# Half of the last gate by TensorE inside the attention stage, and five sums of squares in one PSUM tile

## The chip, the cores and the metric

The kernel runs on one core of one Trainium2 chip. The metric is the device time of one execution in microseconds (us); the fewer the better. PE is the engine of matrix products (TensorE; PEld its loads of stationary operands), DVE the vector engine, ACT the scalar engine, POOL the GpSimd engine; SP issues most of the transfers.

## What is computed

One layer of a hybrid diffusion backbone, in float32, on 512 latent tokens and 128 context tokens (640 rows of 1024 features, handled as five tiles of 128 tokens). Each of the two token kinds has a conditioning vector, and six modulation rows come from it:

```python
mod = (silu(cond) @ w_ada + b_ada)            # w_ada: 1024 x 6144
sh1, sc1, g1, sh2, sc2, g2 = split(mod, 6)
h = rms(x, norm_mix) * (1 + sc1) + sh1
q, k, v, gb, gc, u = split(h @ w_in)          # attention, 8 heads of 64; short convolution
attn = softmax(q_r @ k_all.T / 8) @ v_all     # latents read context and latents
y_conv = gb * conv3(gc * u)
x = x + g1 * (concat(rms(attn), rms(y_conv)) @ w_out)
h2 = rms(x, norm_ffn) * (1 + sc2) + sh2
x = x + g2 * ((silu(gate) * up) @ w_down)     # gate, up = split(h2 @ w_gate_up)
```

The edit concerns `g2`, the last of the six pieces ("section 5" of `w_ada`), and the sums of squares inside `rms(y_conv)`.

## The kernel before

Every float32 product is done as three products of rounded halves (`wh`, `wl` are the high and low part of a weight block, `mH`, `mL` of an activation tile, `hH`, `hL` of the normed input), so a "block" of weights is loaded by a transfer, split by one ACT and one DVE operation, and then used by PE.

The stages, in order of time: first norm and the query projection (0 to about 57 us); keys, values and attention (57 to 256); the output projection in two halves of the columns, `j = 0` and `j = 1` (256 to about 325); the feed-forward part in four groups of blocks (to the end). PE's order is written out by hand: the string `SEQ` lists the steps of the attention stage, where `S`, `T`, `O` are scores, transposes and value products of an attention unit, and `F1` takes one step from a list of fillers. The fillers are the matmuls of the gated convolution, twelve blocks (`gc`, `u`, `gb` for each of four tiles `ct` of channels), six steps each, and between them "ada" steps, which work on the pieces of `w_ada` that are due later. The order on the other engines and on SP's queue is set by a scheduler from dependences and priorities (`early(n)` moves an operation forward).

An ada entry is half a section (512 columns). It takes two ada steps: each uses two blocks `aw` of 512 KB (a ring of two buffers), four matmuls of 32 rows by 512 columns, into one PSUM tile. After the second, ACT copies the tile to `rs`; the next step first turns that into what is needed. For section 2 (`g1`) that is a transfer of the bias row into `rs` and two 128x512 products with `selT`; for sections 3 and 4 four narrow products with `sel`. There were six entries, (2,0) to (4,1); the last of them ends in the output projection, where `next(ada_gen)` and `conv_rms()` are called after the 24 matmuls of the first token tile.

Section 5 (`g2`) was done elsewhere. Its first half took four blocks from the ring `wf`, eight times two operations on DVE (`g2_step(0, ...)`, tile `aacc`) beside the first token tiles of `j = 0`, and after the first tile of `j = 1` two products with `ones` and two additions of the broadcast bias `bb` (`g2_out(0)`). Its second half is done in the same manner in the feed-forward part and stays there.

`conv_rms` makes, for each of five token tiles, one product of `ysum` with a column of ones into a PSUM tile of tag `c` (two buffers in that stage), then scale and add on DVE and a power on POOL.

PSUM has eight banks. The attention stage has tags `t` 2, `c` 3, `o` 1 and `s` (two banks) 1; the output projection `t` 2, `c` 2, `s` 2 of two banks each. In `j = 1`, tile by tile: 24 matmuls, then `h2_turn` of the tile before (eight transposes of `x2n`), while ACT, DVE and POOL carry the projected tile through `mix`, `x2`, its sum of squares and `x2n`.

Of the kernel before, what the change touches and what calls it, by code (L numbers as in the profile page):

```python
# [9 lines left out]
F32 = mybir.dt.float32  # L10
# [5 lines left out]
P = 128  # L16
# [3 lines left out]
NT = 5  # L20
# [39 lines left out]
G2P = -300  # L60
CRP = '0e'
# [30 lines left out]
def build(ctx, tc, x_prompt, x_sample, c, cache_k, cache_v, c_ctx, norm_mix, norm_ffn, w_ada, b_ada,  # L92
# [66 lines left out]
    def rstd_of(ss, n, scale, extra=None, tag="rs"):  # L159
        """(ss * scale + eps) ** -0.5 (times extra)"""  # L160
        w = ss.shape[1]
        ms = T("ms", (P, w), F32, 4)
        dve.tensor_scalar(ms, ss, scale, EPS, ALU.mult, ALU.add)
        r = T(tag, (P, w), F32, 6)
        pool.tensor_tensor(r, ms, neghalf[:, :w], ALU.pow)
        if extra is not None:
            dve.tensor_scalar_mul(r, r, extra)
        return r

    open_pool("A", "left", "")  # L170
    open_pool("F", "right", "of y oz ysum m0 g1 rs5 cp")
    open_pool("H", "right", " ".join(f"hH{k} hL{k}" for k in range(KD)))
    open_pool("B1", "left", "t2 tab selT identr ck cv")
# [21 lines left out]
    def op_load(e):  # L195
        """one stationary operand of a gate and up block: a quarter of the block, or a sum of quarters"""
        f, name = e[0][1:]
        g, u = (order[place[x, f]][5] for x in "gu")
        a11, a12, a21, a22 = g[:, 0:4], g[:, 4:8], u[:, 0:4], u[:, 4:8]
        if name[0] == "S":  # L200
            if name == "S1":
                sums[f] = T("sx", (P, 2, 4, P), F32, 2)
            s13, s24 = sums[f][:, 0], sums[f][:, 1]
            src, x, y, op = {"S1": (s13, a21, a22, ALU.add), "S2": (s24, s13, a11, ALU.subtract),
                             "S3": (s13, a11, a21, ALU.subtract), "S4": (s24, a12, s24, ALU.subtract)}[name]
            with early(SOP[f >= NPLAIN]):
                (pool if f < SPO else dve).tensor_tensor(src, x, y, op)
        else:
            src = {"A11": a11, "A12": a12, "A21": a21, "A22": a22}[name]
        w = T(("wh", "wl")[ops[0] % 2], (P, 2, 4, P), F32R, WHB)  # L210
        ops[0] += 1
        with early(SOP[f >= NPLAIN]):
            split(w[:, 0], w[:, 1], src)
        e[5] = w
# [53 lines left out]
    ADA = [(2, 0), (2, 1), (3, 0), (3, 1), (4, 0), (4, 1)]  # L268
# [6 lines left out]
    for n, (off, ct) in enumerate(CONV + [(None, 0)]):  # L275
        if off is not None:
            plan(("conv", off, ct), wi[:, :, off + ct * P:off + (ct + 1) * P])
        for sec, j, h in ada_steps[2 * n:2 * n + 2 if off is not None else None]:
            col = sec * D + j * 512
            plan(("ada", sec, j, h), wa[:, 2 * h:2 * h + 2, col:col + 512], 1, "a")  # L280
    for j in range(2):
        for kp in range(4):
            plan(("o", j, kp), wo[:, 2 * kp:2 * kp + 2, j * 512:(j + 1) * 512], 2 * j, "w", V_AON + 2 * kp)
        for kp in range(0 if j else 4):
            plan(("ada", 5, j, kp), wa[:, 2 * kp:2 * kp + 2, 5 * D + j * 512:5 * D + (j + 1) * 512], 2, "f")
# [32 lines left out]
    def ada1_load(k):  # L318
        """w_ada of feature tile k of the first norm's scale and shift"""
        out = []  # L320
        for h in range(2):
            wf = T("af", (P, 4, 2, P), F32, AFB)
            for i, col in enumerate((D + k * P, k * P)):
                sp.dma_start(wf[:, :, i], wa[:, 4 * h:4 * h + 4, col:col + P])
            out.append(wf)
            yield
        ada1[k] = out
        yield
# [42 lines left out]
    # products with the two conditions: four contraction tiles at a time on the four column groups of the  # L371
    # array, each with its conditions in the first columns; the groups' sums are added by sel afterwards
# [12 lines left out]
    def vec_do():  # L385
        vps = PB((P, 64))
        pe.transpose(vps, rows, ident[:64, :64])
        dve.tensor_copy(vec[:, 0:64], vps)
        # (1 + b_sc) * norm for both norms
        for i, (bo, no) in enumerate(((8, V_MIX), (32, V_FFN))):  # L390
            dve.scalar_tensor_tensor(nb[:, i], vec[:, bo:bo + KD], 1.0, vec[:, no:no + KD], ALU.add, ALU.mult)

# [4 lines left out]
    def mod_evict(i, f0, n, ps_sc, ps_sh):  # L397
        """ps_*: [P, n, 2] sums without bias for features f0..f0+n tiles"""
        no = (V_MIX, V_FFN)[i]
        bo = (0, 24)[i]  # L400
        if ps_sc is not None:
            tmp = T("modt", (P, n, 2), F32, 2)
            dve.tensor_tensor(tmp, ps_sc, vec[:, no + f0:no + f0 + n].unsqueeze(2).to_broadcast([P, n, 2]), ALU.mult)
            dve.tensor_tensor(modA[i][:, f0:f0 + n, :], tmp,
                              nb[:, i, f0:f0 + n].unsqueeze(2).to_broadcast([P, n, 2]), ALU.add)
        if ps_sh is not None:
            dve.tensor_tensor(modB[i][:, f0:f0 + n, :], ps_sh,
                              vec[:, bo + f0:bo + f0 + n].unsqueeze(2).to_broadcast([P, n, 2]), ALU.add)

# [24 lines left out]
    def xT_do(t):  # L434
        """the normed tokens of tile t, feature-major"""
# [144 lines left out]
    def head_norm(ps, nh, t, which):  # L580
        """rms over each head, gain, rotary; ps [P, nh*64] -> SBUF f32 [P, nh, 64]"""
# [86 lines left out]
    # (chunk, columns of the chunk, token columns, columns of the padded row)  # L668
# [17 lines left out]
    def conv_steps(ct):  # L686
# [22 lines left out]
        for i, _ in enumerate(conv_mm(O_GB, ct, bps)):  # L709
            for j, sc, st, sz in PIECES:  # L710
                if i % 3 == 2 and j == i // 3:
                    s1 = slice(sz.start - 1, sz.stop - 1)
                    dve.tensor_tensor(t1[:, s1], bps[j][:, sc], t1[:, s1], ALU.mult)
            yield
        ysq = ysum if ct == 0 else T("c25", (P, PADW), F32, 3)[:, :PADW - 2]
# [6 lines left out]
    def ada_all():  # L722
        for sec, j in ADA:
# [10 lines left out]
            if sec == 2:  # L734
                sp.dma_start(res[2:3], b_ada[0:1, sec * D + j * 512:sec * D + (j + 1) * 512])
            yield
            if sec == 2:
                for cc in range(2):
                    ps = PB(tag="c")
                    pe.matmul(ps, selT[:, cc], res, start=True, stop=True)  # L740
                    act.activation(g1[cc][:, j * 512:(j + 1) * 512], ps, AF.Copy)
# [18 lines left out]
    def conv_rms():  # L760
        for t in range(NT):
            sps = PB((P, 1), tag="c")
            c0 = t * P + (2 if t == CTX else 0)
            pe.matmul(sps, ysum[:, c0:c0 + P], ones[:, 0:1], start=True, stop=True)
            rB[t] = rstd_of(sps, 1, 1.0 / 512, tag="rB")

    filler = itertools.chain(*(conv_steps(ct) for ct in range(4)), ada_some(12))
    NFILL = 12 * 6 + 12
# [76 lines left out]
    def att_add(t, v, e):  # L845
        # the rows of the v lo products go to the other half of the partitions
# [13 lines left out]
    # the context tokens' queries: four heads at a time  # L860
# [82 lines left out]
    open_pool("D", "right", "mix mH mL aacc bb")  # L943
    phase[0] = 2

# [34 lines left out]
    def g2_step(j, kp):  # L980
        """a quarter of g2's columns: sums over the contraction on the vector engine, then over partitions"""
        w = W(("ada", 5, j, kp))
        for i in range(2):
            k = 2 * kp + i
            for cc in range(2):
              with early(G2P) if G2P and j == 0 else ExitStack():
                if k == 0:
                    g2acc[cc] = T("cg", (P, TOK), F32, 2)[:, :512] if j else T("aacc", (P, 512), F32, 2)
# [4 lines left out]
    def g2_out(j):  # L993
        cols = slice(j * 512, (j + 1) * 512)
        bb = T("cu", (P, TOK), F32, 2)[:, :512] if j else T("bb", (P, 512))
# [6 lines left out]
    # second operands of the gate and up products: quarters of h2 (contraction half, token half) and their sums  # L1002
# [34 lines left out]
    for j in range(2):  # L1037
        cols = slice(j * 512, (j + 1) * 512)
        for n, t in enumerate(TORD[j]):
# [22 lines left out]
            if j == 0 and G2N <= n < 4 + G2N:  # L1062
                g2_step(0, n - G2N)
            if j == 1 and n == 0:
                g2_out(0)
# [18 lines left out]
    # ---- SwiGLU: a gate block and its up block by half the contraction against half the tokens, seven products  # L1084
    # for the eight (Winograd's form) ----
# [16 lines left out]
    def plain(f, bs, toks):  # L1102
        """gate and up blocks of one half of the tokens by plain products"""
# [173 lines left out]
def _rope_constants():  # L1277
    """cos and signed sin of the axial angles, [512 tokens, 64]: they depend on the shapes alone"""
# [37 lines left out]
```

## Time and profile before

| | us |
|---|---|
| median of 3 runs (lowest, highest) | 772.96 (770.6, 773.28) |
| span of the profiled execution, first to last instruction | 771.6 |
| PE busy | 744.2 (96%) |
| DVE busy | 563.1 (73%) |
| ACT busy | 376.8 (49%) |
| POOL busy | 70.8 (9%) |

The profile is of one execution. Its span is 771.6 us; no time of its own beside that is recorded, so what lies around the span is known only as the 1.4 us between it and the median of the runs. The views read here are the shares of the engines, the table by stretches of time (busy time of each engine, granted clock of PE, share and rate of the transfers), the timeline, the chain that ended last, and the answers by tile. In a row of the timeline stand start, duration, engine, line, operation, output and inputs, size and count, and in brackets how long the engine had been idle before it and who ended that.

### The profile page before, as it was taken

To read this page: it belongs to the slowest core of one execution; us is meant where nothing else is said; L and a number is where in the kernel's file an instruction comes from. 1 tells how busy PE (TensorE), PEld (TensorE's weight loads), DVE (VectorE), ACT (ScalarE), POOL (GpSimd) and SP (SyncE) were. 2 spreads that over 40 slices of the span, in tenths; PEclk is the share of its full clock that TensorE was granted. 3 is DMA by queue.
4 is the path that set the end of the run, shared out by engine and by line. 5 is a ranking of instruction groups with operands and counts; after the bars stand their busy time and mean duration, and the time that the engine had idled before them with its cause. 6 is when DMAs were issued, how large, how long until landed. Compare 5 with 4: busy or idle time off the path is not lost.

```text
span 771.6 us, 11961 instructions
## 1 busy us (share of the span) xinstructions
PE 744.2 (96%) x4580; PEld 669.2 (87%) x4580; DVE 563.1 (73%) x1033; ACT 376.8 (49%) x732; POOL 70.8 (9%) x97
## 2 busy tenths in 40 slices
PE   4999999999999999996999999999999999999997
PEld 3778988989999787886998789999889998899986
DVE  5566887675666799789778777984677866788653
ACT  5446676666665346875452125554125542255510
POOL 3105101011010330044100000000000000000000
PEclk9999999999999999999899999999999999999999
DMA  9984134424325433111134412233112231222312
GB/s 290 308 236 128 42 109 140 121 90 140 120 89 171 161 133 110 56 55 55 56 110 153 134 55 83 83 109 110 54 56 82 83 109 56 80 84 84 110 55 82
DMA packets 102350, 84.53 MB, mean 110 GB/s; under 512 B 4526, under 2 KB 82674, under 8 KB 102292
## 3 DMA queue, kind: packets, MB, share of 16 engines
q1 hardware_dynamic: 100980, 83.39, 35.0%
q8 instruction: 36, 0.59, 0.3%
q10 hardware_dynamic: 1056, 0.26, 0.2%
q0 software_dynamic: 256, 0.11, 0.1%
q14 instruction: 22, 0.18, 0.1%
HBM read 79.68 MB, written 2.75 MB: 107 GB/s over the span
## 4 chain that ended last, share of the span: by engine, by line
PE 83%; DVE 8%; ACT 3%; DMA 2%; issue 2%; SPq 2%; POOL 1%; ACTq 0%; POOLq 0%
PE pf L155 17%; PE pf L157 17%; PE pf L156 17%; PE pc L678 3%; PE pc L679 3%; PE pc L680 3%; PE ps L155 3%; PE ps L156 3%; PE ps L157 3%; PE po L833 2%; PE ps L790 2%; PE pt L816 2%; PE pc L380 2%; DMA af<-in_w_ada_dram 2%; DVE wl L152 1%
## 5 line engine op out<-in xcount | busy, mean ns | idle before, releaser
L151 ACT ACTIVATE wh<-wf 128x1024 fp32r<-128x1024 f32 (+1 forms) x76 | 64.1, 843 | 93.1 <-PE pf L157 63.2
L155 PE MATMUL pf<-wh,gH 128*128 128x512 f32 (+1 forms) x225 | 88.2, 392 | 0.0
L157 PE MATMUL pf<-wh,gL 128*128 128x512 f32 (+1 forms) x225 | 87.7, 390 | 0.0
L156 PE MATMUL pf<-wl,gH 128*128 128x512 f32 (+1 forms) x225 | 87.7, 390 | 0.0
L152 DVE TENSOR_TENSOR wl<-wf,wh 128x1024 fp32r<-128x1024 f32 (+1 forms) x42 | 49.4, 1176 | 27.8 <-ACT wh L151 24.9
L678 PE MATMUL pc<-hH,wh 128*128 128x320 f32 x192 | 61.7, 321 | 0.0
L679 PE MATMUL pc<-hL,wh 128*128 128x320 f32 x192 | 60.0, 312 | 0.0
L680 PE MATMUL pc<-hH,wl 128*128 128x320 f32 x192 | 59.9, 312 | 0.0
L155 PE MATMUL pf<-T,wh 128*128 128x320 f32 x160 | 50.1, 313 | 6.2 <-ACT p L1125 6.2
L155 PEld LDWEIGHTS pf<-wh,gH 128*128 128x128 f32 x225 | 42.3, 188 | 9.8 <-ACT wh L151 0.2
L157 PEld LDWEIGHTS pf<-wh,gL 128*128 128x128 f32 x225 | 42.3, 188 | 9.8
L156 PEld LDWEIGHTS pf<-wl,gH 128*128 128x128 f32 x225 | 42.3, 188 | 9.8 <-issue 0.2
L156 PE MATMUL pf<-T,wh 128*128 128x320 f32 x160 | 49.9, 312 | 0.0
L157 PE MATMUL pf<-T,wh 128*128 128x320 f32 x160 | 49.9, 312 | 0.0
L155 PE MATMUL pf<-T,wl 128*128 128x320 f32 x160 | 49.3, 308 | 0.0
L156 PE MATMUL pf<-T,wl 128*128 128x320 f32 x160 | 49.3, 308 | 0.0
L157 PE MATMUL pf<-T,wl 128*128 128x320 f32 x160 | 49.3, 308 | 0.0
L156 PE MATMUL pf<-B,wl 128*128 128x320 f32 x152 | 47.5, 313 | 0.3 <-DVE B L1020 0.3
L155 PE MATMUL pf<-B,wl 128*128 128x320 f32 x152 | 47.4, 312 | 0.0
L157 PE MATMUL pf<-B,wl 128*128 128x320 f32 x152 | 47.2, 310 | 0.0
L1230 DVE TENSOR_TENSOR dm<-pf,g 128x512 f32<-128x512 f32 (+1 forms) x41 | 27.7, 676 | 22.9 <-PE pf L157 22.9
L151 ACT ACTIVATE wl<-wf 128x512 fp32r<-128x512 f32 x34 | 21.4, 630 | 43.5 <-PE pf L156 36.8
(308 smaller groups left out, 2097.5 us busy)
## 6 DMA issues: line engine op xcount, KB each, us to landing
wf<-in_w_gate_up_dram SPq DMA_DIRECT2D x44, 512.0 KB, 3.8
aw<-in_w_ada_dram SPq DMA_DIRECT2D x24, 512.0 KB, 4.7
wf<-in_w_down_dram SPq DMA_DIRECT2D x20, 512.0 KB, 3.2
wf<-in_w_in_dram SPq DMA_DIRECT2D x18, 512.0 KB, 5.9
af<-in_w_ada_dram SPq DMA_DIRECT2D x32, 256.0 KB, 6.1
x<-in_x_sample_dram SPq DMA_DIRECT2D x8, 512.0 KB, 5.3
wf<-in_w_out_dram SPq DMA_DIRECT2D x8, 512.0 KB, 4.5
wf<-in_w_ada_dram SPq DMA_DIRECT2D x8, 512.0 KB, 3.8
```

The costliest lines, as they stand in the source:

```text
L151: act.activation(hi, src, AF.Copy)
L152: dve.tensor_tensor(lo, src, f32(hi), ALU.subtract)
L155: pe.matmul(out, lh, rh, start=start, stop=False, skip_group_check=more)
L156: pe.matmul(out, lh, rl, start=False, stop=False, skip_group_check=more)
L157: pe.matmul(out, ll, rh, start=False, stop=stop, skip_group_check=more)
L380: pe.matmul(out[CG * g:CG * (g + 1)], cp[:, k], w, start=(k < 4), stop=(k >= KD - 4), skip_group_check=True)
L678: pe.matmul(acc, wh[:, k], hH[k][:, c0:c0 + n], start=(k == 0), stop=False)
L679: pe.matmul(acc, wh[:, k], hL[k][:, c0:c0 + n], start=False, stop=False)
L680: pe.matmul(acc, wl[:, k], hH[k][:, c0:c0 + n], start=False, stop=(k == KD - 1))
L790: pe.matmul(s2[:, g, :320], q, kk[:, v, P + g * 320:P + (g + 1) * 320], start=(i == 0), stop=(i == 1))
L816: pe.transpose(tp[:, i, h], u[3][h][:, kt * P:(kt + 1) * P], ident)
L1230: dve.tensor_tensor(dm, ps[:, :n], g2[cc][:, oc], ALU.mult)
```

## The change

The first half of section 5 becomes a seventh ada entry, `(5, 0)`, done on PE like section 2: its bias row goes into `rs`, and two `selT` products give the first halves of the two `g2` tiles, copied by ACT. To have room for it, two ada steps are added: in the `gb` blocks of the channel tiles in `AMID`, 0 and 1, after the first half of the block, with two more `aw` blocks planned there. So every entry comes earlier, the last ada step now stands just ahead of the output projection, and what follows the first token tile there is the end of entry (5,0) in place of (4,1). The DVE path for that half, its `aacc` and `bb` tiles, its four `wf` loads and its two products with `ones` go. `conv_rms` puts its five sums into one PSUM tile of tag `t` and makes one DVE and one POOL operation of them. `selT` moves to a pool that lives longer.

```diff
+AMID = (0, 1)
-    ADA = [(2, 0), (2, 1), (3, 0), (3, 1), (4, 0), (4, 1)]
+    ADA = [(2, 0), (2, 1), (3, 0), (3, 1), (4, 0), (4, 1), (5, 0)]
...
+    for off, ct in CONV:
+        plan(("conv", off, ct), wi[:, :, off + ct * P:off + (ct + 1) * P])
+        n = 4 if off == O_GB and ct in AMID else 2
+        at += n
+        for sec, j, h in ada_steps[at - n:at]:
             col = sec * D + j * 512
             plan(("ada", sec, j, h), wa[:, 2 * h:2 * h + 2, col:col + 512], 1, "a")
...
-        for kp in range(0 if j else 4):
-            plan(("ada", 5, j, kp), wa[:, 2 * kp:2 * kp + 2, 5 * D + j * 512:5 * D + (j + 1) * 512], 2, "f")
...
                     dve.tensor_tensor(t1[:, s1], bps[j][:, sc], t1[:, s1], ALU.mult)
             yield
+            if i == 2 and ct in AMID:
+                yield from ada_some(1)
...
-            if sec == 2:
+            if sec in (2, 5):
                 sp.dma_start(res[2:3], b_ada[0:1, sec * D + j * 512:sec * D + (j + 1) * 512])
             yield
-            if sec == 2:
+            if sec in (2, 5):
                 for cc in range(2):
                     ps = PB(tag="c")
                     pe.matmul(ps, selT[:, cc], res, start=True, stop=True)
-                    act.activation(g1[cc][:, j * 512:(j + 1) * 512], ps, AF.Copy)
+                    act.activation((g1 if sec == 2 else g2)[cc][:, j * 512:(j + 1) * 512], ps, AF.Copy)
...
     def conv_rms():
+        sps = PB((P, NT))
         for t in range(NT):
-            sps = PB((P, 1), tag="c")
             c0 = t * P + (2 if t == CTX else 0)
-            pe.matmul(sps, ysum[:, c0:c0 + P], ones[:, 0:1], start=True, stop=True)
-            rB[t] = rstd_of(sps, 1, 1.0 / 512, tag="rB")
+            pe.matmul(sps[:, t:t + 1], ysum[:, c0:c0 + P], ones[:, 0:1], start=True, stop=True)
+        r = rstd_of(sps, NT, 1.0 / 512, tag="rB")
+        for t in range(NT):
+            rB[t] = r[:, t:t + 1]
...
-            if j == 0 and G2N <= n < 4 + G2N:
-                g2_step(0, n - G2N)
-            if j == 1 and n == 0:
-                g2_out(0)
```

Three places show how the built orders differ; the names are tiles with their running numbers, a bracket names whose semaphore an instruction waits for.

On PE, the end of the attention stage before: value products `po`, the last ada step (`aw` with `cp`), the last two value products, then the output projection (`ps`, with the context tile `m`).

```order
L833 MATMUL po_3235<-pl_3208,VS_696 128x256
L380 MATMUL pc_3096<-aw_3097,cp_84 32x512 [waits DMAHW6_49]
L380 MATMUL pc_3096<-aw_3097,cp_84 32x512
L380 MATMUL pc_3096<-aw_3101,cp_84 32x512 [waits DMAHW7_49]
L380 MATMUL pc_3096<-aw_3101,cp_84 32x512
L833 MATMUL po_3235<-ph_3214,VS_696 128x256 [waits Activation_49]
L833 MATMUL po_3235<-pl_3215,VS_696 128x256 [waits DVE_49]
L155 MATMUL ps_3297<-wh_3105,m_170_701 128x512 [waits PE_49]
```

The same place on PE now:

```order
L838 MATMUL po_3245<-pl_3225,VS_696 128x256 [waits DVE_49]
L679 MATMUL pc_3235<-hH_40_155,wh_3013 128x320
L680 MATMUL pc_3235<-hL_48_163,wh_3013 128x320
L681 MATMUL pc_3235<-hH_40_155,wl_3014 128x320
L679 MATMUL pc_3235<-hH_41_156,wh_3013 128x320
L680 MATMUL pc_3235<-hL_49_164,wh_3013 128x320
L681 MATMUL pc_3235<-hH_41_156,wl_3014 128x320
L381 MATMUL pc_3130<-aw_3131,cp_84 32x512 [waits DMAHW2_49]
L381 MATMUL pc_3130<-aw_3135,cp_84 32x512 [waits DMAHW3_49]
L156 MATMUL ps_3325<-wh_3139,m_170_701 128x512 [waits DVE_49,Activation_49]
```

And on ACT, the rows from the copy of the last value products (`t`) on:

```order
L845 ACTIVATE t_772_3201<-po_3245 128x256 [waits PE_49]
L249 ACTIVATE wh_3183<-wf_3181,vec_143 128x512 [waits DMAHW4_49,PE_49]
L720 ACTIVATE c_782_3280<-y_699 128x512 [waits DVE_49]
L720 ACTIVATE c_782_3280<-y_699 128x128 [waits DVE_49]
L736 ACTIVATE rs_783_3289<-pc_3130 128x512 [waits PE_49]
L152 ACTIVATE mH_3321<-y_699 128x512
```

The last six convolution matmuls have moved behind the last value products, the ada step stands directly ahead of the output projection, and the first `ps` matmul waits for ACT: its tile takes PSUM banks 0 and 1, and bank 0 holds `pc_3130`, the ada step's sum, until the `rs` copy has read it (before, the sum stood in bank 2).

On PE after the first 24 matmuls of the output projection, before:

```order
L157 MATMUL ps_3297<-wh_3138,mL_3294 128x512
L745 MATMUL pc_3328<-sel_140,rs_774_3253 128x2 x4
L764 MATMUL pc_3336<-ones_130,ysum_700 128x1 [waits Pool_49]
L764 MATMUL pc_3342<-ones_130,ysum_700 128x1 [waits DVE_49]
L764 MATMUL pc_3348<-ones_130,ysum_700 128x1 [waits DVE_49]
L764 MATMUL pc_3354<-ones_130,ysum_700 128x1 [waits DVE_49]
L764 MATMUL pc_3360<-ones_130,ysum_700 128x1 [waits DVE_49,Pool_49]
```

and now:

```order
L158 MATMUL ps_3325<-wh_3183,mL_3322 128x512
L743 MATMUL pc_3395<-rs_783_3289,selT_142 128x512 [waits DMAHW0_49]
L743 MATMUL pc_3398<-rs_783_3289,selT_142 128x512
L767 MATMUL pt_3401<-ones_130,ysum_700 128x1 [waits Pool_49]
L767 MATMUL pt_3401<-ones_130,ysum_700 128x1 x3
L767 MATMUL pt_3401<-ones_130,ysum_700 128x1 [waits Pool_49]
L156 MATMUL ps_3426<-wh_3139,mH_3418 128x512 [waits Activation_49]
```

The four narrow `sel` products are replaced by two full `selT` products, and the sums no longer wait for DVE one by one.

On DVE, the first token tile of `j = 1` on its way to `x2n`, before (`mix` scaled, gated, added to `x`; `g` the two bias additions of `g2_out(0)`):

```order
L1072 SCALAR_TENSOR_TENSOR mix_3658<-ps_3615,rA_2009,mix_3658 128x512 [waits Activation_49]
L1000 TENSOR_TENSOR g_784_3291<-pt_3652,bb_3650 128x512 [waits PE_49]
L1074 TENSOR_TENSOR mix_3658<-mix_3658,g_166_697 128x512 [waits DVE_49]
L1000 TENSOR_TENSOR g_785_3292<-pt_3655,bb_3650 128x512 [waits PE_49]
L1075 TENSOR_TENSOR x_837_3466<-mix_3658,x_837_3466 128x512 [waits DMAHW7_49,DVE_49]
L152 TENSOR_TENSOR mL_3740<-y_699,mH_3739 128x512
L152 TENSOR_TENSOR mL_3818<-of_3032,mH_3817 128x512 [waits PE_49,Activation_49]
L163 TENSOR_SCALAR ms_3666<-ss_3664 128x1 [waits Activation_49]
```

and now:

```order
L1072 SCALAR_TENSOR_TENSOR mix_3630<-ps_3595,rA_2015,mix_3630 128x512 [waits Activation_49]
L153 TENSOR_TENSOR mL_3712<-y_699,mH_3711 128x512 [waits PE_49]
L1074 TENSOR_TENSOR mix_3630<-mix_3630,g_166_697 128x512 [waits DVE_49]
L153 TENSOR_TENSOR mL_3790<-of_3042,mH_3789 128x512 [waits PE_49,Activation_49]
L1075 TENSOR_TENSOR x_829_3460<-mix_3630,x_829_3460 128x512 [waits DMAHW2_49,DVE_49]
L164 TENSOR_SCALAR ms_3638<-ss_3636 128x1 [waits Activation_49]
```

The two additions are gone, and the low half `mL` of a later token tile, which waits for ACT's `mH` of it, now stands ahead of the addition to `x`.

More of the change, by code (lines that the diff above doesn't have):

```diff
@@ L170, in build @@
     open_pool("A", "left", "")
-    open_pool("F", "right", "of y oz ysum m0 g1 rs5 cp")
+    open_pool("F", "right", "of y oz ysum m0 g1 rs5 cp selT")
     open_pool("H", "right", " ".join(f"hH{k} hL{k}" for k in range(KD)))
-    open_pool("B1", "left", "t2 tab selT identr ck cv")
+    open_pool("B1", "left", "t2 tab identr ck cv")
     open_pool("B0", "left", "crow rows rows2 res x xT hF af")
@@ L274, in build @@
     ada_steps = [(sec, j, h) for sec, j in ADA for h in range(4)]
[L275 to L278, printed above, removed]
+    at = 0
+    for off, ct in CONV:
[3 more added lines that the diff above has]
+        for sec, j, h in ada_steps[at - n:at]:
             col = sec * D + j * 512
@@ L760, in conv_rms @@
     def conv_rms():
+        sps = PB((P, NT))
         for t in range(NT):
-            sps = PB((P, 1), tag="c")
             c0 = t * P + (2 if t == CTX else 0)
-            pe.matmul(sps, ysum[:, c0:c0 + P], ones[:, 0:1], start=True, stop=True)
-            rB[t] = rstd_of(sps, 1, 1.0 / 512, tag="rB")
-    filler = itertools.chain(*(conv_steps(ct) for ct in range(4)), ada_some(12))
-    NFILL = 12 * 6 + 12
+            pe.matmul(sps[:, t:t + 1], ysum[:, c0:c0 + P], ones[:, 0:1], start=True, stop=True)
+        r = rstd_of(sps, NT, 1.0 / 512, tag="rB")
+        for t in range(NT):
+            rB[t] = r[:, t:t + 1]
+    filler = itertools.chain(*(conv_steps(ct) for ct in range(4)), ada_some(2 * len(ADA)))
+    NFILL = 12 * 6 + 2 * len(ADA)
     used = [0]
@@ L942, in build @@
     open_pool("Y1", "left", "B11 B21")
-    open_pool("D", "right", "mix mH mL aacc bb")
+    open_pool("D", "right", "mix mH mL")
     phase[0] = 2
@@ L985, in g2_step @@
             for cc in range(2):
-              with early(G2P) if G2P and j == 0 else ExitStack():
                 if k == 0:
-                    g2acc[cc] = T("cg", (P, TOK), F32, 2)[:, :512] if j else T("aacc", (P, 512), F32, 2)
+                    g2acc[cc] = T("cg", (P, TOK), F32, 2)[:, :512]
                     dve.tensor_scalar_mul(g2acc[cc], w[:, i], cs[:, k, cc:cc + 1])
@@ L994, in g2_out @@
         cols = slice(j * 512, (j + 1) * 512)
-        bb = T("cu", (P, TOK), F32, 2)[:, :512] if j else T("bb", (P, 512))
+        bb = T("cu", (P, TOK), F32, 2)[:, :512]
         sp.dma_start(bb, b_ada[0, 5 * D + j * 512:5 * D + (j + 1) * 512].partition_broadcast(P))
```

## The prediction

> **What bounds the kernel now.** I read the page first: the shares of the engines and of the chain that ended last.
>
> ```profile
> span 771.6 us, 11961 instructions
> PE 744.2 (96%) x4580; PEld 669.2 (87%) x4580; DVE 563.1 (73%) x1033; ACT 376.8 (49%) x732; POOL 70.8 (9%) x97
> PE 83%; DVE 8%; ACT 3%; DMA 2%; issue 2%; SPq 2%; POOL 1%; ACTq 0%; POOLq 0%
> ```
>
> PE is the bound: 27 us of the span are without it, and its share of the chain is ten times any other's. So work taken from DVE counts only where PE waits for DVE, and work given to PE counts in full unless PE was idle there. The table by stretches (columns: stretch, length, then busy time and instructions of PE, PEld, DVE, ACT, POOL, granted clock, transfer share, GB/s) says where that is:
>
> ```profile
> 98.00:150.00 52.00, 51.88 (x373) 46.34 (x366) 39.88 (x78) 36.41 (x72) 3.79 (x6) 1.00 0.41 129
> 150.00:200.00 50.00, 49.96 (x367) 45.76 (x366) 31.96 (x66) 30.59 (x62) 5.48 (x9) 1.00 0.32 102
> 200.00:256.00 56.00, 56.00 (x415) 51.20 (x414) 37.42 (x76) 33.45 (x68) 2.41 (x7) 1.00 0.38 124
> 262.00:266.00 4.00, 2.63 (x21) 2.43 (x20) 3.94 (x13) 0.94 (x2) 1.42 (x2) 0.98 0.65 212
> 266.00:270.00 4.00, 4.00 (x12) 3.13 (x12) 2.32 (x6) 0.69 (x1) 2.42 (x4) 0.59 0.87 324
> ```
>
> From 98 to 256, where all ada steps stand, PE idles 0.16 us of 158. Right behind the output projection's first tile it idles 1.37 of 4, and in the next 4 us its clock is 0.59. After 325 nothing changes; that part only shifts.
>
> **A. Two more ada steps, four more narrow products ahead of the projection.** Prices from the chain (start, duration, what):
>
> ```profile
> 158.94 1.72 PE pc L740 x4
> 186.20 0.15 PE pc L680
> 186.35 0.79 PE pc L745 x8
> 187.13 0.99 PE pc L380 x8
> 188.71 0.24 PE po L833 x2
> 273.17 0.79 PE pt L902 x8
> ```
>
> One full ada step (two blocks, eight passes) takes 0.99, two 1.98. The `sel` products of entry (4,1), 0.79, move from behind the projection's first tile into this stretch. PE is full there, so both count whole: **+2.77**.
>
> **A'. New waits in that stretch.** The `aw` ring has two buffers, so a step's loads start only when the step before it has been read. Before, their closest spacing was 12.5 us (rows of SP's queue); by the order now, steps 3 to 4, 6 to 7 and 7 to 8 are some 7.2, 7.5 and 6.3 us apart (24 convolution passes at 0.15, eight to ten `po` passes at 0.12, a step's own 0.99, a few scores and transposes).
>
> ```profile
> 231.77 0.89 SPq L225 DMA_DIRECT2D aw<-in_w_ada_dram  x2
> 244.26 0.89 SPq L225 DMA_DIRECT2D aw<-in_w_ada_dram  x2
> DMA to landing us min/median/max: 3.7/4.7/6.4
> PE ps L790 <- ACT pr L798: 0.6, 1, 0.6
> ```
>
> The second block lands about 0.1 + 0.45 + 4.7 = 5.25 us after the release (half of 0.89 until it is issued; the median landing), 6.95 at the longest landing. It is needed in the middle of the next step, so available are 6.7, 7.0 and 5.8 (the spacings less half of 0.99). So normally no wait; with the longest landing 1.15 and 0.25, together 1.4. Since scores and transposes also shift against each other, three unit waits of the size of the last row (1.8) may come on top: bounds 0 and 3.2 (nothing below 0, since that stretch has only 0.16 us of idle to give back). I take **+0.5**, near the low end, because the median landing leaves no wait.
>
> **B. The first projection matmul waits for ACT.** Its two-bank tile now covers the bank that holds the last ada sum, and is written only when ACT has copied that to `rs`. Before, in the timeline:
>
> ```profile
> 253.64 0.31 PE L680 MATMUL pc<-hH,wl 128*128 128x320 f32 x1
> 253.84 0.72 ACT L248 ACTIVATE wh<-wf,vec 128x512 fp32r<-128x512 f32 x1 [1.68 <-PE pc L679]
> 254.74 0.71 ACT L248 ACTIVATE wh<-wf,vec 128x512 fp32r<-128x512 f32 x1
> 255.35 0.82 ACT L717 ACTIVATE c<-y 128x512 f32<-128x512 f32 x2
> 256.07 0.58 ACT L733 ACTIVATE rs<-pc 128x512 f32<-128x512 f32 x1
> ```
>
> Counted from the last convolution pass (253.64): ACT has the `wh` split from +0.20, the second `wh` from +0.83 (0.63 per split, back to back), the two `c` squares from +1.44 (0.61 later, as 254.74 to 255.35), `rs` from +2.16 (0.72 later, as 255.35 to 256.07), done at +2.74. PE is done with that pass and the ada step at about +1.2 (0.15 and 0.99). So it waits about 1.5 to 1.6: **+1.6**; bounds 0 (`rs` goes ahead of the squares and splits) and 2.0 (one more `wh` row, 0.7, less what overlaps).
>
> **C, D, E. The block of sums behind the projection's first tile.**
>
> ```profile
> 259.20 0.40 PE L156 MATMUL ps<-wl,mH 128*128 128x512 f32 x1
> 259.71 0.50 PE L157 MATMUL ps<-wh,mL 128*128 128x512 f32 x1
> 260.05 0.40 PE L155 MATMUL ps<-wh,mH 128*128 128x512 f32 x1
> 262.15 0.95 PE L745 MATMUL pc<-sel,rs 128*128 128x2 f32 x8
> 264.49 0.60 PE L764 MATMUL pc<-ones,ysum 128*128 128x1 f32 x4 [1.16 <-DVE modt L403]
> 265.30 0.61 PE L764 MATMUL pc<-ones,ysum 128*128 128x1 f32 x4 [0.20 <-DVE ms L163]
> 265.76 0.72 PE L155 MATMUL ps<-wh,mH 128*128 128x512 f32 x1
> 269.26 0.39 PE L157 MATMUL ps<-wh,mL 128*128 128x512 f32 x1
> ```
>
> A `ps` pass at full clock takes 0.233 (nine from 260.05 to 262.15). C: a wait for the first `mL` (259.20 to 259.71, 0.28 more than a pass) ends, since DVE gets it during B: **-0.28**. D: from 262.15 to 265.76 are 3.61 us. Now stand there two `selT` products, 1.72, and ten ones-passes at 0.79/8 = 0.099, 0.99, which share one PSUM tile and wait for no DVE: 2.71, so **-0.90** (bounds -0.9 and, if the first `selT` product waits for the bias row's transfer, up to 0). E: from 265.76 to 269.26 eight passes take 3.50 instead of 8 x 0.233 = 1.87, the low clock after the narrow block. With PE denser there: **-1.63** (bounds -1.63 and 0).
>
> **F. First tile of `j = 1`.**
>
> ```profile
> 296.39 1.88 PE L999 MATMUL pt<-aacc,ones 128*128 128x512 f32 x4
> 300.92 0.63 ACT L151 ACTIVATE mH<-of 128x512 fp32r<-128x512 f32 x1 [3.36 <-issue]
> 301.46 1.04 ACT L1080 ACTIVATE x2n<-x 128x1024 f32<-128x1024 f32 x1
> 301.59 0.69 DVE L152 TENSOR_TENSOR mL<-of,mH 128x512 fp32r<-128x512 f32 x1 [0.24 <-ACT mH L151]
> 304.25 1.09 PE L961 MATMUL pt<-ident,x2n 128*128 128x128 f32 x8 [0.37 <-DVE x2n L1082]
> 305.10 0.48 PE L155 MATMUL ps<-wh,mH 128*128 128x512 f32 x1
> ```
>
> Let T be the end of tile 0's matmuls (296.39). Before, the matmuls of tile 2 begin at T+8.71. The products with `ones` are gone (1.72 by the `selT` row), so PE has tile 1 done at T+5.6 (24 x 0.233). But the chain to `x2n` isn't shorter by that: DVE now has `mL` of a later tile ahead of the addition to `x`; it waits for ACT's `mH`, which comes after the 11th matmul of tile 1, at T+2.8 (before, 300.92 = T+4.53, the same 1.72 later). So `mL` from T+3.5, the addition from about T+4.1, ACT's square from T+4.84, the transposes 2.79 later (301.46 to 304.25) at T+7.63, the next matmuls 0.85 after that (304.25 to 305.10), T+8.48: **-0.23**, with a new wait of PE of about 2.0 in place of 1.72 of work and 0.37 of wait. Without `mL` in front it would be about T+6.5; bounds -2.1 (work and wait both gone) and 0.
>
> **G. Off the path, 0:** the 16 DVE products into `aacc` and two bias additions, four short powers on POOL, four `wf` transfers that become four `aw` transfers of the same size on the same queue, the broadcast bias that becomes one row.
>
> ```profile
> L991 DVE SCALAR_TENSOR_TENSOR aacc<-wf,cs,aacc x14: 735/742/1772, 258.3 to 280.6; 128x512 f32<-128x512 f32 x14
> ```
>
> Twelve us of DVE, but from 258 to 281 PE waited for DVE only in the places above; PE's own work covers it, and were it not covered, it would cost nothing to be without it.
>
> **Sum:** 2.77 + 0.5 + 1.6 - 0.28 - 0.90 - 1.63 - 0.23 = +1.83. The profiled span 771.6 becomes 773.4; the median, 1.4 above that span, becomes 772.96 + 1.83 = **774.8**. It is a small sum of larger terms: what is won in the transition is paid in the attention stretch and in two new waits. Half a per cent, 3.9 us, is about what a measurement of this kernel can tell from no change.
>
> **A rule against the rows: the clock.** The rows of E show a drop after 1.36 us of waits within 3.6 us of narrow products. One more place shows it:
>
> ```profile
> 72.00:74.00 2.00, 1.15 (x9) 0.87 (x9) 2.00 (x11) 1.74 (x5) 0.70 (x1) 1.00 0.24 70
> 74.00:76.00 2.00, 2.00 (x13) 2.00 (x14) 1.65 (x5) 1.83 (x5) 0.80 (x1) 0.67 0.00 0
> ```
>
> PE was idle 0.85 of 2 us here, and the clock fell to 0.67. So a drop can follow B (1.6 idle) or F (2.0 idle and eight transposes). The Trainium skill, "TensorE: Matmul & The Clock Gate", section "HAM oscillation — how this bites in real kernels", has as its rule that the array must have no idle gap above some 3.4 us; by that rule neither B nor F lowers the clock and the sum stays at +1.83. Both rows above disagree with it as it stands, since these gaps were shorter; by them the sum could be +3.46.
>
> **Rivals.**
> R1, the low clock comes back at one of the new waits: E's 1.63 is not won (or is paid again), 774.8 + 1.63 = 776.4. For it: the rows at 72 and 266. Against: full matmuls stand on both sides of B and F. Chance 0.22.
> R2, the ada steps arrive late, the other side: the short spacing makes them wait for loads (1.4) and three units slip (1.8), 2.7 above the 0.5 taken: 777.5, slower. It decides from 2.0 above my sum, where 776.8 is passed. For it: spacing down from 12.5 to 6.3 with no third buffer. Against: the median landing. Chance 0.13.
> R3, the waits of B and F don't appear, since ACT gets to `rs` sooner and `x2n` is done as early as PE is free: -1.6 and, to T+6.5 for the transposes' end, some -1.1: 772.1. For it: neither wait is seen in this trace, and both rest on an order of queues. Against: that order is fixed, and the durations are measured. Chance 0.18.
> R1 with R2: 779.1, chance 0.05.
> My forecast, 774.8: 0.42.
>
> **Numbers.** Forecast and R3 and most of R1 lie within 3.9 us: same 0.74. Slower, R2, R1 with R2 and the upper part of R1: 0.23. Faster needs 769.1, below R3; it takes R3 with F's lower bound: 0.03. Range 771.8 (just below R3) to 778.2 (above R2); beyond it are R1 with R2 and an R3 at its bounds, the forecast with another sign of A', under 0.2 in all.
>
> **What would show it.** The stretch up to the projection longer by about 2.8 us with PE still full and waits of ada steps for `aw` under 1.4 in all (A, A'). A wait of about 1.6 before the first `ps` pass, ended by ACT's `rs` copy (B). No waits between the ones-passes, clock 1.0 behind them (D, E). A wait of about 2 us before tile 0's `x2n` transposes, with DVE's `mL` ahead of the addition (F). Wrong I'd be by a clock below 0.9 behind B or F, or by a sum of `aw` waits above 2.

## The result, and the profile after

| | before | after |
|---|---|---|
| median, us (lowest to highest) | 772.61 (770.6 to 773.28) | 779.32 (778.89 to 780.97) |
| span of the profiled execution, us | 771.6 | 778.0 |

The ratio of the times is 1.0085, with a 95% interval of 1.0063 to 1.0107: the kernel became 6.7 us slower, 0.85%. The forecast was 774.8 with a range to 778.2, so the time lies above it.

The page of after, the three lines that answer to those shown of before:

```profile
span 778.0 us, 11967 instructions
PE 747.3 (96%) x4596; PEld 668.5 (86%) x4596; DVE 551.5 (71%) x1011; ACT 378.9 (49%) x735; POOL 66.5 (9%) x93
PE 79%; DVE 9%; ACT 4%; DMA 3%; POOL 2%; issue 2%; SPq 1%; ACTq 0%; DVEq 0%; POOLq 0%
```

DVE has lost 11.6 us of work, as the edit says. PE is busy 3.1 us longer and idle 3.3 us longer, and the chain shows it: four points have gone from PE to DVE, ACT, DMA and POOL. Where is read from the table by stretches. I cut it at the same instructions in both kernels, the first `aw` step and the first `ps` pass of the output projection (first row before, the others after; columns as in the prediction):

```profile
97.79:256.18 158.39, 158.22 (x1154) 143.64 (x1153) 109.66 (x218) 100.85 (x204) 11.75 (x23) 1.00 0.37 119
```

```profile
96.40:264.48 168.08, 163.84 (x1177) 145.40 (x1177) 111.39 (x221) 102.41 (x207) 11.39 (x23) 1.00 0.39 124
72.00:76.00 4.00, 3.02 (x24) 2.74 (x25) 4.00 (x16) 3.56 (x10) 1.37 (x2) 1.00 0.12 35
306.00:310.00 4.00, 2.06 (x11) 1.42 (x10) 2.12 (x5) 2.24 (x4) 0.55 (x1) 1.00 0.00 0
310.00:314.00 4.00, 4.00 (x16) 3.43 (x15) 3.67 (x13) 3.39 (x9) 0.00 (x0) 0.57 0.00 0
```

The stretch grew by 9.69 us, where the prediction had 4.87 (A, A' and B). PE's idle in it went from 0.17 to 4.24. The waits of PE in after, from 96 us to the end of the projection (who waited, for whom; total, times, longest):

```profile
PE pt L966 <- DVE x2n L1082: 1.9, 1, 1.9
PE ps L156 <- ACT rs L736: 1.5, 1, 1.5
PE ps L795 <- ACT pr L803: 1.2, 3, 0.6
PE pc L381 <- ACT c L693: 0.7, 1, 0.7
PE pt L821 <- DVE pl L153: 0.6, 1, 0.6
```

The first two are F and B of the prediction. The other three belong to the attention stage, and none of them is for a transfer: `pr` and `pl` belong to the units, and the ada step that waits for `c` waits for a PSUM buffer that ACT has still to read. Of the 1.2 us for `pr`, one wait of 0.59 ends at 95.6 us, ahead of the stretch; before had the same one there (0.56).

How a unit came to wait is seen at one place. Before, timeline, PE, from the first eight transposes of a unit to its last two:

```profile
157.91 1.04 PE L816 MATMUL pt<-ident,pr 128*128 128x128 f32 x8
158.78 1.88 PE L740 MATMUL pc<-rs,selT 128*128 128x512 f32 x4
160.59 1.06 PE L380 MATMUL pc<-aw,cp 128*32 128x512 f32 x8
161.59 0.44 PE L816 MATMUL pt<-ident,pr 128*128 128x128 f32 x2
```

The same unit after, with DVE:

```profile
160.68 1.03 PE L821 MATMUL pt<-ident,pr 128*128 128x128 f32 x8
161.47 0.39 PE L679 MATMUL pc<-hH,wh 128*128 128x320 f32 x1
162.49 1.28 DVE L153 TENSOR_TENSOR pl<-pt,ph 128x512 fp32r<-128x512 f32 x2
163.23 0.44 PE L821 MATMUL pt<-ident,pr 128*128 128x128 f32 x2 [0.64 <-DVE pl L153]
```

Before, 2.8 us of filler (two `selT` products and an ada step) stood between the two groups of transposes, and DVE's `pl` had emptied the PSUM buffer in time. After, the filler that falls here is six convolution passes, 0.9 us; DVE has emptied it only at about 163.2, and PE waits 0.64. The long filler has moved to another unit, which had shown no wait without it.

The start of the output projection (B), the block of sums (C to E) and the first tile of `j = 1` (F), timeline of after:

```profile
261.94 1.06 PE L381 MATMUL pc<-aw,cp 128*32 128x512 f32 x8
263.85 0.57 ACT L736 ACTIVATE rs<-pc 128x512 f32<-128x512 f32 x1
264.48 0.50 PE L156 MATMUL ps<-wh,m 128*128 128x512 f32 x1 [1.48 <-ACT rs L736]
```

```profile
270.19 1.88 PE L743 MATMUL pc<-rs,selT 128*128 128x512 f32 x4
271.90 1.17 PE L767 MATMUL pt<-ones,ysum 128*128 128x1 f32 x10
272.93 0.48 PE L156 MATMUL ps<-wh,mH 128*128 128x512 f32 x1
274.89 0.40 PE L158 MATMUL ps<-wh,mL 128*128 128x512 f32 x1
```

```profile
305.51 0.69 DVE L153 TENSOR_TENSOR mL<-of,mH 128x512 fp32r<-128x512 f32 x1 [0.34 <-ACT mH L152]
306.12 0.68 DVE L1075 TENSOR_TENSOR x<-mix,x 128x512 f32<-128x512 f32 x1
309.74 1.69 PE L966 MATMUL pt<-ident,x2n 128*128 128x128 f32 x8 [1.94 <-DVE x2n L1082]
311.08 0.78 PE L156 MATMUL ps<-wh,mH 128*128 128x512 f32 x1
```

The wait for the copy to `rs` is 1.48, the block takes 2.74 (270.19 to 272.93), eight passes behind it take 1.96 in place of 3.50, and PE waits 1.94 for `x2n`, with `mL` ahead of the addition to `x`. Behind that last wait the granted clock fell to 0.57 (310 to 314), and the transposes and the passes after them took some 1.6 us longer. Against this, the low clock that before had from 74 us on is missing (72 to 76 at 1.00), though PE's instructions there are the same.

### The profile page after: what moved, and what is told of

The parts are those of the page before. It is cut to its first block, busy times and chain, and to the rows that moved or that the text cites. A ratio compares the mean times of both kernels' runs of the same rounds, so it can differ in the third digit from the quotient of the medians.

```text
span 778.0 us, 11967 instructions
## 1 busy us (share of the span) xinstructions
PE 747.3 (96%) x4596; PEld 668.5 (86%) x4596; DVE 551.5 (71%) x1011; ACT 378.9 (49%) x735; POOL 66.5 (9%) x93
## 4 chain that ended last, share of the span: by engine, by line
PE 79%; DVE 9%; ACT 4%; DMA 3%; POOL 2%; issue 2%; SPq 1%; ACTq 0%; DVEq 0%; POOLq 0%
PE pf L156 17%; PE pf L158 17%; PE pf L157 17%; PE pc L679 3%; PE ps L156 3%; PE pc L680 3%; PE pc L681 3%; PE ps L157 3%; PE ps L158 3%; PE po L838 2%; PE ps L795 2%; PE pc L381 2%; DMA af<-in_w_ada_dram 2%; PE pt L821 2%; POOL rs L166 1%
```

## The experiments

Each was timed in five rounds beside the kernel before; the ratio is to that kernel, with its 95% interval. After itself has 1.0085 [1.0063, 1.0107].

**The shift alone.** The kernel before, with two empty steps:

```diff
+            if i == 2 and ct in (0, 1):
+                yield
...
-    NFILL = 12 * 6 + 12
+    NFILL = 12 * 6 + 14
```

> The kernel before, with all its work, but with two empty filler steps (nothing is done in them) where the change puts its two added ada steps. So every later convolution and ada step stands one or two places later against the attention units, as in the change, and the last six convolution passes and the last ada step stand behind the last value products. Theory 1 (the loss is the displacement: PE's fillers no longer cover the softmax of the units they were placed for): the attention stretch gets some 4 to 5 us longer by waits of single units, and the wait for the copy to rs of 1.5 us appears; 772.6 + 5.5 = about 778. Rival (the loss is the added work, its loads, and its waits for PSUM): only the 1.5 us in front of the output projection appear, about 774.

Measured: 779.29 us, ratio 1.0075 [1.0054, 1.0096]. Its stretch from the first `aw` step to the projection, and PE's waits in it:

```profile
98.87:264.45 165.58, 161.41 (x1154) 144.23 (x1153) 111.39 (x219) 101.81 (x206) 11.38 (x23) 1.00 0.35 114
```

```profile
PE ps L155 <- ACT rs L735: 1.5, 1, 1.5
PE pt L818 <- DVE pl L152: 0.7, 1, 0.7
PE po L835 <- DVE pl L152: 0.6, 2, 0.3
```

The same 1154 passes as before take 165.58 in place of 158.39: 7.2 us longer with nothing added, and 1.48 of that is B. Of the rest, 5.7, some 2.5 is idle that before didn't have (2.7 in place of 0.17); the other 3.2 is longer busy time of the same passes. Most of it stands at the recorded waits themselves, for a wait costs more than its idle: in after the last of the six convolution passes starts at 162.29 and the transposes behind it at 163.23, 0.94 where such a pass takes 0.15, with 0.64 recorded as idle. Counted so, from start to start, the ten unit waits of this run that before didn't have come to some 4.8 of the 5.7 (an estimate from its timeline).

Two kinds of wait have to be told apart. Seven of the ten stand where they stand in after too, most with nearly the same size, as the first row here (0.67; in after 0.64). The other two rows stand where the second empty step is; there after has `sel` products and an ada step, and no wait:

```profile
162.37 0.44 PE L818 MATMUL pt<-ident,pr 128*128 128x128 f32 x2 [0.67 <-DVE pl L152]
172.71 0.39 PE L835 MATMUL po<-ph,VS 128*128 128x256 f32 x1 [0.25 <-ACT ph L151]
173.44 0.38 PE L835 MATMUL po<-pl,VS 128*128 128x256 f32 x1 [0.34 <-DVE pl L152]
```

So about 1 us of this run's loss comes from the step being empty, which the change doesn't have, and the wait of 0.7 us for `c` in after isn't in this run. With that said, the shift is enough to make most of the loss, and it costs more than the added work.

**The added steps without a place of their own.**

```diff
-            yield
-            if i == 2 and ct in AMID:
-                yield from ada_some(1)
+            if i == 2 and ct in AMID:
+                list(ada_some(1))
+            yield
...
-    NFILL = 12 * 6 + 2 * len(ADA)
+    NFILL = 12 * 6 + 2 * len(ADA) - len(AMID)
```

> The change, but each of the two added ada steps is done within the filler step ahead of it and takes no place of its own, so every convolution pass stands against the attention units where it did before. All the work is the same. Theory 1 (displacement): waits in the attention stretch fall from about 5 us to about 1, and the wait ahead of the output projection becomes 0 to 0.8; 779.3 - 4 - 1 = about 774. Rival (added work and loads cost by themselves): 777.5 to 779.

Measured: 777.9 us, ratio 1.0069 [1.0044, 1.0094]: my theory missed by 4 us, and the time is that of the rival. The stretch, a part of it, and its waits:

```profile
96.42:264.73 168.31, 164.19 (x1178) 146.79 (x1177) 110.20 (x220) 101.21 (x206) 12.28 (x23) 0.99 0.39 123
228.00:232.00 4.00, 2.79 (x22) 2.71 (x20) 2.07 (x5) 1.29 (x4) 0.00 (x0) 1.00 0.08 25
232.00:236.00 4.00, 4.00 (x20) 3.96 (x21) 1.41 (x3) 2.42 (x5) 0.70 (x5) 0.58 0.00 0
```

```profile
PE pt L907 <- ACT osq L861: 1.2, 1, 1.2
PE pt L821 <- DVE pl L153: 1.1, 1, 1.1
PE ps L795 <- ACT pr L803: 0.8, 1, 0.8
```

The convolution passes stand where they stood, B is down to 0.4, and still units wait, 3.5 us in all with a wait of 0.4 that the list leaves out, and a low clock follows one of the waits. So the place of the convolution passes isn't all that the loss hangs on. The two steps with an added ada step are longer by it, and what this edit doesn't put back is the ada entries: with two more steps ahead of them, every entry after the first comes a step or two earlier, and with it the long fillers (`selT` 1.7, `sel` 0.8). "Displacement" would have to be taken wider than I had put it: any filler of another length at a unit's gap. That the entries are what is left was not tried by itself. By this run alone the rival, that the added work costs by itself, would stand; what speaks against it is e1, which loses without added work, and e5 below, which has all of it and loses little.

**The sums alone,** on the kernel before: only the new `conv_rms`.

```diff
+        sps = PB((P, NT))
         for t in range(NT):
-            sps = PB((P, 1), tag="c")
...
+        r = rstd_of(sps, NT, 1.0 / 512, tag="rB")
```

> The kernel before with only the other part of the change, the five sums of squares in one PSUM tile. The two waits of PE for DVE (1.36 us) and, if they cause it, the low clock behind them (1.63 us) go: 772.6 - 2.8 = about 769.8. Rival (the drop of the clock comes from the narrow products and not from the waits): 771.3.

Measured: 769.47 us, ratio 0.9955 [0.9939, 0.997]. In before, the longer of PE's two waits in this block (1.16 us) was for `modt`, which on DVE stood behind two products into `aacc`:

```profile
262.94 1.42 DVE L991 SCALAR_TENSOR_TENSOR aacc<-wf,cs,aacc 128x512 f32<-128x512 f32 x2
264.27 0.16 DVE L403 TENSOR_TENSOR modt<-pc,vec 128x8 f32<-128x8 f32 x1
```

The two stretches in which before had 1.37 us of idle and a clock of 0.59, now:

```profile
262.00:266.00 4.00, 4.00 (x28) 3.64 (x27) 3.93 (x10) 0.94 (x2) 0.88 (x1) 1.00 0.51 153
266.00:270.00 4.00, 4.00 (x19) 3.21 (x18) 2.87 (x4) 1.31 (x2) 2.35 (x2) 1.00 0.92 369
```

Both are gone, though the same ten narrow passes and eight `sel` passes are still there: the waits, not the narrow products, caused the low clock. (No profile here of a kernel with the new sums has a low clock at this place.) This half of the change is worth 3.5 us, and alone it is the fastest version that computes everything.

**The old sums in the change.**

```diff
-        sps = PB((P, NT))
         for t in range(NT):
+            sps = PB((P, 1), tag="c")
...
+            rB[t] = rstd_of(sps, 1, 1.0 / 512, tag="rB")
```

> The change with the sums of squares done as before, one PSUM tile and one pair of DVE and POOL operations each. If the edit of the sums is what ended waits and low clock there, this costs 1.4 to 3 us: 780.7 to 782.3. Rival (taking the aacc work off DVE alone ended the waits): within 0.5 us of 779.3.

Measured: 781.85 us, ratio 1.011 [1.0087, 1.0134]; its interval overlaps that of after, so the 2.5 us are likely but not shown. In its profile:

```profile
272.85 0.38 PE L767 MATMUL pc<-ones,ysum 128*128 128x1 f32 x2 [0.25 <-DVE ms L164]
273.48 1.08 PE L767 MATMUL pc<-ones,ysum 128*128 128x1 f32 x6 [0.25 <-DVE ms L164]
```

0.5 us of waits in place of 1.36, and no low clock behind them in that execution. What is gone is the wait for `modt`: in this kernel neither `modt` nor the `aacc` products ahead of it stand there. Which of the two it was, this run doesn't separate.

**The added steps later:** `AMID = (2, 3)` in place of `(0, 1)`.

> The change with the two added ada steps in the gb blocks of channel tiles 2 and 3 in place of 0 and 1, so the fillers are shifted only from about 190 us on. If the loss is the displacement of fillers against the units, the waits before 190 us (1.5 to 3 us of them) go: about 776.5. If it is the work, its loads or its PSUM tile by themselves: within 0.7 of 779.3.

Measured: 773.54 us, ratio 1.0022 [1.0008, 1.0035]: 5 us are back by two numbers. Stretch and the one longer wait of a unit in it:

```profile
97.58:260.67 163.09, 161.92 (x1177) 144.97 (x1177) 110.59 (x220) 101.51 (x204) 12.12 (x22) 1.00 0.40 128
```

```profile
PE po L838 <- DVE pl L153: 1.0, 1, 1.0
```

All the work is the same; the stretch is 4.70 longer than before's, of which 2.77 are the added products. The units wait less, the ada step's wait for `c` is gone, and so is B: in this order the first `ps` pass starts before ACT's copy. The last ada step does come up against its load here: it takes 1.38 us in place of 0.99. The time is 3 us better than I had expected; half of that is B, which I had left in.

**The addition to `x` first:** `XP = 200` in place of `50`.

> The change with a higher priority for the operations between the projection's sum and x2n, so that DVE does the first tile's addition to x in j = 1 ahead of the low half of a later token tile. Step F of the prediction: the wait of PE for x2n (1.9 us) falls to about 0.6, and if the low clock behind it comes from that wait, 1.6 us of that go too: 779.3 - 1.3 - 1.6 = 776.4 with, 778 without the clock. Rival (the x2n chain is long for another reason): within 0.5 of 779.3.

Measured: 778.04 us, ratio 1.0078 [1.0059, 1.0098]; the time can't tell this from after. The profile can: the wait is down from 1.94 to

```profile
PE pt L966 <- DVE x2n L1082: 0.6, 1, 0.6
```

and no low clock follows it.

**The half on PE within the projection,** on the sums-only kernel. Two of the eight products by token tile, in place of the DVE steps; the bias row and two `selT` products as in the change:

```diff
+        if j == 0:
+            if kp == 0:
+                g2acc[0] = PB(tag="c")
+            for i in range(2):
+                cond_mm(g2acc[0], 2 * kp + i, w[:, i])
```

> The kernel before with the sums in one PSUM tile, and the first half of section 5 on PE, but within the output projection: two passes of 32 rows by token tile of j = 0 in place of the DVE steps, and two selT products after the first tile of j = 1 in place of the two products with ones. The attention stage is as before. If the added work costs only its own time and the rest of the loss was displacement: sums-only kernel 769.5 + 2.0 - 0.4 (the wait for x2n) = about 771. If work for that half costs more than its passes wherever it is put: 775 or more.

Measured: 773.23 us, ratio 1.0015 [1.0001, 1.0029], 2 us above what I expected. The attention stretch is that of before, 158.33 with 0.17 idle. The missing 2 us are the products themselves:

```profile
264.30 1.05 PE L380 MATMUL pc<-wf,cp 128*32 128x512 f32 x4
265.28 0.50 PE L155 MATMUL ps<-wh,mH 128*128 128x512 f32 x1
```

Four passes of 32 columns take 0.98 here, as long as eight in an ada step (0.99). In a step they go to all four groups of 32 columns of the array, one behind the other; two matmuls alone fill two groups, and the time is not halved. Four such pieces cost 3.9 us in place of 2.0: 769.5 + 3.9 = 773.4, near what was measured. The Trainium skill, "TensorEngine Tiling (Array Packing)", section "Theoretical Speedup", gives up to four times for a small dimension of 32. The rows show a part of that, twice the work in the same time with four groups as with two; the four times no run here shows.

**The half not done at all,** on the sums-only kernel, which shows what there was to win. The first halves of `g2` are the bias alone, so this kernel leaves a part of the result out.

```diff
-                g2_step(0, n - G2N)
+                pass
...
+        if j == 0:
+            for cc in range(2):
+                sp.dma_start(g2[cc][:, cols], b_ada[0, 5 * D:5 * D + 512].partition_broadcast(P))
+            return
```

> The kernel before with the sums in one PSUM tile, and without the product for the first half of section 5 at all (the first halves of g2 are the bias alone; its four loads, 16 DVE operations, two products with ones and two additions are left out). It bounds what taking that half away can bring. Step F: the chain to x2n then sets the time, so nearly nothing of the 1.72 + 0.37 us comes back: 769.2, or 770.8 with a low clock behind the new wait. Rival (work and wait both go): 767.4.

Measured: 768.52 us, ratio 0.9961 [0.9948, 0.9973]: no gain over the sums alone (0.9955). The products with `ones` are gone, and in their place stands

```profile
PE pt L963 <- DVE x2n L1088: 1.9, 1, 1.9
```

**The same with the addition to `x` first** (`XP = 200`).

> The kernel without the first half of section 5 (as e8, the first halves of g2 are the bias alone), and with the higher priority of e6, so that the addition to x stands ahead of the later tile's low half. If step F holds (what was saved on PE there is waited for again, by the order on DVE), the saving now comes out: the wait for x2n falls from 1.9 us to about 0.6 and the low clock behind it goes, 768.5 - 1.3 to 2.9 = 765.6 to 767.2. Rival: as e8, 768.5.

Measured: 766.47 us, ratio 0.9934 [0.9914, 0.9954]; the wait for `x2n` is 0.6. It lies within the 765.6 to 767.2 of the theory; against e8 the intervals just overlap. So step F has its mechanism: what PE saved there came back as a wait, by the order on DVE. With the order turned the half does have a price: the same priority with the half still on DVE (e12 below) takes 770.17, ratio 0.9981 [0.9962, 1.0001], and these two intervals don't overlap, though 1.2 us of that difference is a wait that e12 has of its own.

**The copy to `rs` first:** `with early(300) if sec == 5` around it, which puts it ahead of the two squares.

> The change with ACT's copy to rs of the entry (5,0) ahead of the two squares that stood in front of it. Step B: the wait ahead of the output projection falls from 1.5 us to about 0.3 (two squares of 0.6 fewer): 779.3 - 1.2 = 778.1. Rival (the time comes back at the next wait of that stage, the low half of the first tile or the bias row): within 0.3 of 779.3.

Measured: 778.04 us, ratio 1.0085 [1.0063, 1.0107], the same as after. In the profile the wait fell by half only,

```profile
PE ps L156 <- ACT rs L736: 0.8, 1, 0.8
```

0.7 us, which is under what these runs tell.

**Both repairs,** `AMID = (2, 3)` and `XP = 200`, and **the sums with `XP = 200`.**

> e5 and e6 together: the two added ada steps in channel tiles 2 and 3, and the addition to x first. If the two repairs add, 773.5 - 1.3 = 772.2; still above the kernel with the sums alone (769.5), since the 3 us of added PE work stay.

> The kernel before with the sums in one PSUM tile and the higher priority of e6, everything else as before: a try for the fastest version. The wait for x2n there is only 0.4 us: 769.2, between 768.8 and 769.6.

Measured: 773.25 us, ratio 1.0019 [1.0004, 1.0034], not to be told from e5; and 770.17 us, 0.9981 [0.9962, 1.0001], not better than the sums alone. In the latter the higher priority brought a new wait of PE for a weight block's low half:

```profile
PE ps L156 <- DVE wl L249: 1.2, 1, 1.2
```

## Why the prediction was wrong, point by point

**A, right.** The added products cost their full price: in after an ada step takes 0.99 (172.37 to 173.36), eight `sel` passes 0.89 (171.48 to 172.37, in another place than the 0.79 of the prediction). After less shift-alone, 9.69 - 7.19 = 2.5 us of stretch, is near the 2.77 too, but by luck in part, since each of the two has a wait that the other hasn't.

**A', the step that failed.** I took 0.5 us, with bounds of 0 and 3.2. The stretch grew by 9.69; less B (1.48) and A (2.77) remain 5.4. Two things were wrong in it. First the cause: I worked out loads of `aw` that might come late. The steps did come as close as I had them (7.7, 7.7 and 6.5 us apart), but in after no ada step waited for a load. Second the bound: I had named units that shift, but "three unit waits of 0.6" had no working behind it; I had one row of such a wait in before, which stands at 97.0 us, ahead of the stretch, and took its size for the size of a shift that touches the units from about 123 us, the first added step, to the end. I also priced a wait by its idle alone, and it costs some 0.2 us more (about 4.8 for 2.5 of idle in the ten waits of e1). The row that spoke was the other one: 0.16 us of idle in 158. As I read it now, PE's order there fits ACT and DVE so closely that a filler's length often stands for a wait that isn't there. The shift alone (e1) costs 5.7, about 1 of it by its empty step; starting the shift later (e5) leaves 1.9 (4.70 less 2.77). Some 0.8 of the 5.4 is the wait for `c`, which came with the added work and not with the shift. Which of the shifted fillers cost how much stays open, as e2 shows.

**B, right.** 1.48 for 1.6. **C and D, right:** from the first `ps` pass to the end of the block 9.58 became 8.45, -1.13 for -1.18. **E, right,** and shown as a thing of the waits by e3.

**F, right in the chain, wrong in the clock of this execution.** The wait of about 2 us came (1.94), by the order I gave (e6, e8, e9). Behind it the clock fell, which cost some 1.6 us: rival R1. It isn't in every execution: of the six profiles here with a wait of 1.8 or 1.9 at this place three show the drop (after, e2, e8) and three don't (e4, e5, e10).

**G, right:** taking the DVE work and its loads away brought nothing by itself (e8), though the two products with `ones` went with them. What there was to win lay in F, behind the order on DVE (e9).

With 5.4 for 0.5 in A', the sum would have been +6.7, and the median rose by 6.7 us. That it fits to a tenth is luck in part: R1's price was in the profile too, but so was a low clock of before at 74 us (1.4 us) that after didn't have, and the two cancel in the spans. Of the rivals, R1 came in the profiled execution, and R2 by half: its units that slip came, at about three times the 1.8 us, and its late loads didn't. R1 with R2 gave 779.1, next to the 779.3 measured, but 1.4 of that is loads that nobody waited for; the number is met by luck.

## What to carry to other kernels

In a stage where the bound engine shows no idle, fillers placed by hand are part of the schedule: before adding one, count how many later ones it moves against the work they cover, and price that shift by each moved gap, not by the waits that the old order shows. Try the shift with an empty step, minding that the empty place can make a wait of its own, and try another place before giving up the change: here two numbers brought back 5 of 6.7 us. And ask first what the removed work can bring, by leaving it out: here nothing as DVE's order stood, and some 3 us once that order was turned too (769.5 to 766.5, with intervals that overlap), while the small edit beside it (five sums in one tile) was the whole gain.

## What the hardware showed that I had not expected

The clock falls after less idle than I would have thought, and not each time. PE idle 0.85 of 2 us (before, at 72), 1.37 of 4 (before, at 262), 1.21 of 4 (e2, at 228) and 1.94 of 4 (after, at 306) were each followed by 4 us or so at 0.57 to 0.67; at 72 to 76 after had 0.98 of 4 us idle and kept 1.00, and e4 had 1.85 of 4 (308 to 312, the wait for `x2n`) and kept it too. The Trainium skill, "TensorE: Matmul & The Clock Gate", section "HAM oscillation — how this bites in real kernels", asks for no idle gap above some 3.4 us; these gaps are shorter, so the measurement decides. A drop cost about 1.5 us here (1.54 at E, 1.6 at F, 1.4 at 74 us), and removing the waits (e3) removed the one at E.

Products of 32 columns have no price each: eight passes over four column groups took 0.99 us, four over two groups 0.98.
